# A hybrid decoder step on one core: which place the planner charges for a large tile, and four PSUM banks in turn for the side work

## The chip, the cores and the metric

The kernel runs on one core of one Trainium2 chip. The metric is the device time of one execution in microseconds (us). Lower is better.

## What is computed

Two decoder layers run over 1,024 prompt tokens and 64 sample tokens (8 sequences of 8), in 32-bit floats. The model width is 1,024 and each of the four branches is 512 wide. Cut to what matters, one layer is:

```python
h = rmsnorm(x, norm_w[l])
proj = h @ w_in[l]          # a_x a_b a_c a_z  s_u s_z  c_q c_f c_i c_z  d_q d_k d_v d_z d_r  m_logit
y_a = a_b * short_conv(a_c * a_x, st_conv[l], conv_w[l]) * silu(a_z)
y_s, h_r, h_i = s5_ssm(s_u, ...)                 # 32 groups, 64 complex states each, scan over time
sg = gelu(y_s)
y_b = sg * sigmoid(sg @ w_glu[l] + b_glu[l]) * silu(s_z)
o_c, S_c = gated_recurrence(q_c, k_c, v_c, logf_c, st_hg[l])      # HGRN2, 4 heads, chunks of 64
y_c = rmsnorm(o_c, hgrn_norm[l]) * silu(c_z)
o_d, S_d = gated_recurrence(q_d, k_d, v_d, gk, st_gla[l])         # GLA, 4 heads
y_d = rmsnorm(o_d, gla_norm[l]) * silu(d_z)
p = einsum('blnw,nwd->blnd', stack([y_a, y_b, y_c, y_d]), w_branch[l])
x = x + sum_n(sigmoid(m_logit) * p) @ w_out[l]
```

A final RMSNorm follows, and all end states of the branches are outputs too.

## The kernel before

**Products.** A 32-bit product is made of three TensorE matmuls over operands split into a high and a low part (high times high, low times high, high times low): `xh`, `xl` or `hi`, `lo` on one side, `whi`, `wlo` on the other. ACT makes the high part and DVE the low part. TensorE thus is the engine with by far the most work. A *unit* is one block of 128 output columns over all 1,088 tokens: `unit` runs it as two halves, each of which is 4 accumulations of 272 tokens in two PSUM banks, 48 matmuls over the model width or 24 over a branch's. In the first part of a layer the units go in pairs with seven block products in place of eight (`pair`, names `xc`, `top`, `spot`, `wsum`); the merge gate's pairs are the last of these.

**Stages of a layer.** Projections for the convolution and for S5 (early units and pairs), then the gate pairs, under which the S5 lane runs in four rounds. Then the heads in the order `ORDER = 'H0 H1 H2 H3 G0 G1'`, under which the two recurrences run. Then the merge, in the order `STAGES = '0 2 U 1 3'`: the branch products of the convolution and of HGRN2, the half-GLU of S5 (`U`), the branch products of S5 and of GLA; then `out_proj`. In the profiled execution the gate pairs with the S5 lane lie at about 350 to 760 us (layer 0) and 1840 to 2270 us (layer 1), the heads and the merge at 760 to 1350 and 2270 to 2865 us.

**Lanes.** Everything that is not a unit's matmul is written as generators, the lanes `aux`, `s5l`, `tabs` and `rec`. At each `yield` a lane says when its operands are ready, how many PSUM banks the next step takes (`nsm`), how many large tiles (`need`) and a condition.

**What sets the order.** The program is written once by a planner. `Book` keeps an account of when each engine is free and when each tile was last written and read; `enter` adds a price for every instruction. Between two matmuls of a unit, `Trunk.pump` asks each lane whether its next step is ready by the account, whether the PSUM banks are free by the account (`bank`), whether enough large tiles are left (`fits`), and whether DVE's account is no more than `backlog` ahead of TensorE's (12 us, in the gate pairs 0.5 us). If so the step is written there, and stands in each engine's queue at that place. What the account has wrong becomes a wait on the chip, since every engine works through its own queue in order.

**Places.** Large tiles (128 x 1088 words) come from a pool `big` of `NBIG = 38` places. Before, the account does not know which place a new tile takes: a tile whose place is still being read is written as if it were free. The PSUM has 8 banks: two single ones for the lanes (tag `sm`) and three pairs for the units (tag `mm`).

**Names in the rows.** One helper records every instruction, so nearly all rows of the trace have line L88, and tiles tell them apart. In an S5 round, POOL makes `tm<-Ppow,s5b`, then `et<-tm`, twice, then small products `qp`, `qt` and a memset of `tm`; DVE makes `tm<-Ppow,s5pk` and `gt<-tm`, later copies `tm<-s5b`; TensorE transposes `et` (copied out to `E`) and multiplies `sm<-s5b,tm` and `sm<-gt,tm`, later `sm<-H,gt` and `sm<-apad,E`. In the recurrences `pr`, `prh`, `prl`, `prs`, `att`, `k`, `Tb` and `apad` belong to the decay and attention steps, `osq`, `sqh`, `sql` to the norm of a head's output `o`. In the merge `y` is a branch's output, `g` the gate and `mg` the sum; `yv` and its parts `xh`, `xl` feed the half-GLU.

Of the kernel before, what the change touches and what calls it, by code (L numbers as in the profile page):

```python
# [9 lines left out]
F32 = mybir.dt.float32  # L10
# [16 lines left out]
NBIG = 38  # L27
# [17 lines left out]
WBUF = 5  # L45
KEEP = 5
SPARE5 = 6
LEAD = 0.7


TURNS = (-2, 5, 11)
# [8 lines left out]
SEM = 0.05  # L60
# [36 lines left out]
class Book:  # L97
    def __init__(self, nc):
        self.nc = nc
        self.free = dict.fromkeys(("pe", "act", "dve", "pool", "sp", "dma"), 0.0)  # L100
        self.wr, self.rd = {}, {}
        self.table = None
        for attr, key in (("tensor", "pe"), ("scalar", "act"), ("vector", "dve"), ("gpsimd", "pool"), ("sync", "sp")):
            setattr(self, attr, Meter(self, getattr(nc, attr), key))

    def enter(self, key, op, aps, func):
        out, ins = aps[0], aps[1:]
        n = 1
        for d in max((x.shape[1:] for x in aps), key=lambda d: math.prod(d)):
            n *= d  # L110
        free, us = self.free, 1e-3
        parts = [self.parts_of(x) for x in aps]
        wr = [max(self.wr.get(k, 0.0) for k in p) for p in parts]
        rd = [max(self.rd.get(k, 0.0) for k in p) for p in parts]
        start = max([free[key]] + [t + SEM for t in wr[1:]])

        if key == "pe":
            start = max(start, rd[0] + SEM)
        else:
            start = max(start, rd[0] + SEM, wr[0] + SEM if op != "dma_start" else 0.0)  # L120
        if op == "dma_start":
            free[key] = start + (0.75 if key == "pool" else 0.45)
            size = math.prod(out.shape) * 4.0
            free["dma"] = max(free["dma"], free[key]) + size / 350e3
            end = free["dma"] + 1.9
        else:
            if key == "pe":
                m = math.prod(aps[-1].shape[1:]) if op == "matmul" else 128
                c = (m / 2400 + 0.011 if aps[1].dtype == F32R else 2 * max(m / 1200 + 0.004, 0.109)
                     if op == "matmul" else 0.11)  # L130
            elif key == "act":
                c = 0.155 + n * 0.87 * us
                if func in TABLED and func != self.table:
                    self.table = func
                    c += 1.3
            elif key == "dve":
                c = 0.15 + n * 1.05 * us
            else:
                c = 0.4 if n < 128 else 0.15 + n * (2.4 if op.startswith("tensor_t") or op in ("tensor_mul", "tensor_add", "tensor_sub")
                               else 0.9) * us  # L140
            free[key] = end = start + c
        for p in parts[1:]:
            for k in p:
                self.rd[k] = max(self.rd.get(k, 0.0), end)
        for k in parts[0]:
            self.wr[k] = end

    @staticmethod
    def parts_of(x):

        n = x.name
        if n[:2] not in ("xh", "xl", "hi", "lo", "sp") or getattr(x, "offset", None) is None:
            return (n,)
        a, size = x.offset % T, math.prod(x.shape[1:])
        return ((n,) if a < HT else ()) + ((n + "b",) if a + size > HT else ())
# [16 lines left out]
class Trunk:  # L172
    def __init__(self, ctx, tc, a, o):
# [9 lines left out]
        self.n = 0  # L183
        self.lanes = []
        self.banks = []
        self.alive = set()
        self.keep = KEEP
        self.backlog = BACKLOG
        self.inside = None
# [17 lines left out]

    def bank(self, n):

        names = self.banks[-2:][:n]  # L210
        return max([max(self.nc.rd.get(x, 0.0), self.nc.wr.get(x, 0.0)) + SEM for x in names] + [0.0])

    def free(self, *aps):
        for x in aps:
            self.alive.discard(x.name)

    def fits(self, ln):
        if ln.when and not ln.when():
# [3 lines left out]
    def pump(self):  # L222
        again = True
        while again:
            again = False
            self.weights()
            for ln in self.lanes:
                if (ln.q and ln.ready <= self.now and self.bank(ln.nsm) <= self.now and self.fits(ln)
                        and self.nc.free["dve"] <= self.now + self.backlog):
                    self.stage(ln)  # L230
                    again = True
                    break
# [33 lines left out]
    def big(self, shape, dt=F32, name="b"):  # L266
        n = 1
# [6 lines left out]
        v = t[:shape[0], :n]  # L274
        self.alive.add(v.name)
        assert len(self.alive) <= NBIG, sorted(self.alive)
        if len(shape) == 2:
            return v
        names = "abcdef"[: len(shape) - 1]
        return v.rearrange(f"p ({' '.join(names)}) -> p {' '.join(names)}", **dict(zip(names, shape[1:])))  # L280

    def sm(self):
        t = self.ps.tile([128, 512], F32, tag="sm", name=self.nm("sm"))
        self.banks.append(t[:].name)
        return t

    def mm(self):
        return self.ps.tile([128, 2, 512], F32, tag="mm", name=self.nm("mm"), bufs=3)

    @staticmethod  # L290
    def cut(t, span, nb):
# [61 lines left out]
    def parts_by(self, j):  # L353
# [38 lines left out]
                src = a22  # L392
                drop = [e + 2]

        old = self.places[-WBUF:][0] if len(self.places) >= WBUF else ()
        yield 1, max([self.at(src[:])] + [nc.rd.get(x, 0.0) + SEM for x in old])
        hi = self.wp.tile([128, 4, 128], F32R, tag="whi", name=self.nm("whi"), bufs=WBUF)
        lo = self.wp.tile([128, 4, 128], F32R, tag="wlo", name=self.nm("wlo"), bufs=WBUF)
        self.places.append((hi[:].name, lo[:].name))
        h, lv, r = hi[:], lo[:], src[:]  # L400
        if perm in (1, 2):
            h, lv = (x.rearrange("q k (p g) -> q k g p", g=8) for x in (h, lv))
# [311 lines left out]
    def make_plan(self):  # L714
        self.plan, self.seq = [], []
        self.loaded, self.done, self.raws, self.ws, self.sums_ = set(), set(), {}, {}, {}
        self.nraw = self.di = self.wi = 0
        self.preps, self.places = [], []
        self.merging = False
        self.left = [0.0] * RAWS  # L720

# [411 lines left out]
    def recurrence(self, l, nh, q, f, k, v, vs, sz, y_dst, nw_col, s0, sp_out, ss_out, gate=None):  # L1133
# [24 lines left out]
            Ah = [(A[:, hh, :], hs) for hh, hs in enumerate(heads)]  # L1158
            self.free(q)
        B = k  # L1160
        yield self.at(*own[1]), 0
        own, ready = self.parts(own, cuts, heads)
        yield ready, 1, 1

# [48 lines left out]
        for _ in adv:  # L1213
            pass
        self.free(f)
        yield self.at(*pair[1]), 0
        pair, ready = self.parts(pair, cuts, heads)
        yield ready, 1
        for hh, hs in enumerate(heads):
# [149 lines left out]
        for hh in range(nh):  # L1369
# [22 lines left out]
            for c in cuts:  # L1392
                nc.vector.tensor_mul(sq[:, c], o[:, c], o[:, c])
                nc.scalar.activation(hi[:, c], o[:, c], AF.Square)
            yield self.at(hi), 0
            _, ready = self.parts((sq, (hi, lo)), cuts, heads[:1] if nh == 1 else [slice(0, 128)])
            self.alive.add(sq.name)
            yield ready, 1
            for s, n in SP:
                p = self.sm()  # L1400
# [5 lines left out]
            if len(sz) <= hh:  # L1406
                yield 0.0, 0, 0, lambda: len(sz) > hh
            nc.scalar.activation(sq, sq, AF.Exp, scale=-0.5)
            yield self.at(sq), 0
            nc.vector.tensor_mul(o, o, sq)  # L1410
            nc.vector.scalar_tensor_tensor(o, o, self.cols[:, nw_col:nw_col + 1], sz[hh], op0=ALU.mult, op1=ALU.mult)
            yield self.at(o), 0
# [6 lines left out]
    def gla_gate(self, l, pr):  # L1419
# [22 lines left out]
            yield 0.0, 1  # L1442
        nc.scalar.activation(f, f, AF.Exp, scale=-1.0)
        nc.scalar.activation(f, f, AF.Ln, bias=self.ones[:])
        yield self.at(f), 0
        nc.vector.tensor_sub(f, m, f)
        nc.scalar.activation(f, f, AF.Exp, scale=1.0 / 16.0)
        self.free(m)
# [770 lines left out]
    def layer(self, l):  # L2219
# [38 lines left out]
        self.keep = KEEP  # L2258
        self.backlog = BACKLOG
        self.more = True  # L2260
        for op in ORDER.split():
            i = int(op[1:] or 0)
            if op[0] == "H":
                self.hgrn_units(l, i)
            elif op[0] == "m":
                if i not in sum(early, []):
                    self.gate_unit(l, i)
            else:
                self.gla_units(l, i)
        self.merge(l)  # L2270
        self.mg_h = self.mg
        self.out_proj(l)

# [41 lines left out]
```

## Time and profile before

| | us |
|---|---|
| median of 3 runs | 3059.04 (3057.76 to 3060.28) |
| the profiled execution | 3063.25 |
| span of its trace | 3061.3 |
| busy in it: TensorE | 2947.9 (96%) |
| busy in it: DVE | 1931.8 (63%) |
| busy in it: ACT | 1110.3 (36%) |
| busy in it: POOL | 389.6 (13%) |

All rows below come from the profiled execution, which took 4.2 us more than the median. In the rows, PE is TensorE, PEld its weight loads; "PEclk" is the clock that the throttle granted to TensorE as a share of 2.4 GHz, so that 0.50 is the lower of its two levels (1.2 GHz). In a timeline a row is a start, a busy time, the instruction, the number of merged instructions, and in brackets the idle time of the engine before it and what ended that.

### The profile page before, as it was taken

The numbers are of one execution on the slowest core, as the hardware profiler recorded it, in microseconds if no ns is written. First come the engines' busy times: TensorE is split into PE (matmuls) and PEld (weight loads), VectorE is DVE, ScalarE is ACT, GpSimd is POOL, SyncE is SP. The second block draws the span as 40 slices with busy tenths as digits, with TensorE's granted clock in tenths as the row PEclk, the third lists the DMA queues.
The fourth block names the chain that finished last, engine by engine and source line by source line (L and its number), as shares of the span: only waits on it lengthen the run. The fifth ranks groups of instructions, "written<-read, shape, count | busy, mean of one in ns | idle before, by whom it ended". The sixth has DMA issues, their size and how long they took to land.

```text
span 3061.3 us, 55591 instructions
## 1 busy us (share of the span) xinstructions
PE 2947.9 (96%) x22890; PEld 2862.4 (94%) x22890; DVE 1931.8 (63%) x3396; ACT 1110.3 (36%) x1932; POOL 389.6 (13%) x432
## 2 busy tenths in 40 slices
PE   7999999999999999989999999999999999999998
PEld 6999899999999999989889999999899999999997
DVE  5776676775656466868455666777645565577662
ACT  5332433333333426243343243333333344344321
POOL 2000202220000020213010002211100000103120
PEclk9999999999999999999999999999999999999999
DMA  4422333334212115435233223333421221245332
GB/s 119 162 71 61 101 111 107 106 97 143 61 47 66 40 39 183 153 102 195 88 128 107 62 72 118 100 102 110 162 63 47 63 67 37 75 160 159 133 136 89
DMA packets 318609, 309.41 MB, mean 101 GB/s; under 512 B 18497, under 2 KB 269649, under 8 KB 318357
## 3 DMA queue, kind: packets, MB, share of 16 engines
q1 hardware_dynamic: 316516, 302.02, 31.3%
q0 software_dynamic: 1840, 3.86, 0.4%
q8 instruction: 180, 2.95, 0.4%
q14 instruction: 73, 0.59, 0.1%
HBM read 217.16 MB, written 88.65 MB: 100 GB/s over the span
## 4 chain that ended last, share of the span: by engine, by line
PE 81%; DVE 7%; issue 4%; ACT 3%; DMA 2%; POOL 1%; SPq 1%; DVEq 0%; POOLq 0%; ACTq 0%
PE mm L88 70%; PE sm L88 11%; DVE wlo L88 1%; SPq L88 1%; ACT whi L88 1%; DMA apad<-usc 1%; DVE att L88 1%; DVE spot L88 1%; POOL et L88 1%; POOL tm L88 0%; DVE yb L88 0%; ACT L88 0%; DMA s5b<-in_s_b_im_dram 0%; DVE gt L88 0%; DVE wsum L88 0%
## 5 line engine op out<-in xcount | busy, mean ns | idle before, releaser
L88 PE MATMUL mm<-xc,whi 128*128 128x272 f32 x3136 | 526.7, 290 | 8.9 <-DVE spot L88 7.9
L88 PEld LDWEIGHTS mm<-xc,whi 128*128 128x128 f32 x3136 | 445.4, 191 | 12.7 <-issue 5.8
L88 DVE TENSOR_TENSOR wlo<-wraw,whi 128x512 fp32r<-128x512 f32 x400 | 315.8, 792 | 215.4 <-ACT whi L88 214.4
L88 PE MATMUL mm<-hi,whi 128*128 128x272 f32 (+2 forms) x1928 | 410.9, 293 | 12.5 <-ACT hi L88 4.3
L88 PE MATMUL mm<-lo,whi 128*128 128x272 f32 (+2 forms) x1928 | 409.5, 292 | 4.8 <-DVE lo L88 4.8
L88 PE MATMUL mm<-hi,wlo 128*128 128x272 f32 (+2 forms) x1928 | 409.2, 292 | 0.4 <-DVE wlo L88 0.4
L88 PE MATMUL mm<-xh,whi 128*128 128x272 f32 (+1 forms) x1720 | 370.5, 295 | 9.1 <-ACT spot L88 3.4
L88 PE MATMUL mm<-xl,whi 128*128 128x272 f32 (+1 forms) x1720 | 367.3, 293 | 11.7 <-DVE xl L88 11.7
L88 PE MATMUL mm<-xh,wlo 128*128 128x272 f32 (+1 forms) x1720 | 367.8, 294 | 3.4 <-DVE wlo L88 3.4
L88 ACT ACTIVATE whi<-wraw 128x512 fp32r<-128x512 f32 x400 | 272.8, 686 | 155.9 <-PE mm L88 124.2
L88 PE MATMUL mm<-xc,wlo 128*128 128x272 f32 x1568 | 326.6, 290 | 0.0
L88 PEld LDWEIGHTS mm<-hi,whi 128*128 128x128 f32 x1928 | 306.8, 191 | 15.8 <-issue 5.2
L88 PEld LDWEIGHTS mm<-lo,whi 128*128 128x128 f32 x1928 | 306.5, 191 | 7.1 <-DVE lo L88 5.8
L88 PEld LDWEIGHTS mm<-hi,wlo 128*128 128x128 f32 x1928 | 306.0, 191 | 2.6 <-issue 1.2
L88 PEld LDWEIGHTS mm<-xl,whi 128*128 128x128 f32 x1720 | 274.4, 191 | 13.4 <-DVE xl L88 12.7
L88 PEld LDWEIGHTS mm<-xh,whi 128*128 128x128 f32 x1720 | 274.3, 191 | 12.4 <-ACT whi L88 3.9
L88 PEld LDWEIGHTS mm<-xh,wlo 128*128 128x128 f32 x1720 | 273.9, 191 | 6.5 <-DVE wlo L88 5.3
L88 PEld LDWEIGHTS mm<-xc,wlo 128*128 128x128 f32 x1568 | 247.6, 190 | 0.7 <-issue 0.7
L88 ACT ACTIVATE whi<-wsum 128x512 fp32r<-128x512 f32 x147 | 99.4, 677 | 205.3 <-DVE wsum L88 172.1
L88 DVE TENSOR_TENSOR spot<-spot,mm 128x544 f32<-128x544 f32 x181 | 129.6, 716 | 53.3 <-PE mm L88 50.7
L88 ACT ACTIVATE spot<-spot 128x544 f32<-128x544 f32 x87 | 57.4, 660 | 266.2 <-DVE spot L88 264.6
L88 DVE TENSOR_TENSOR wlo<-wsum,whi 128x512 fp32r<-128x512 f32 x147 | 114.1, 776 | 54.5 <-ACT whi L88 53.3
(367 smaller groups left out, 5162.9 us busy)
## 6 DMA issues: line engine op xcount, KB each, us to landing
wraw<-in_w_in_dram SPq DMA_DIRECT2D x328, 256.0 KB
g<-gsc SPq DMA_DIRECT2D x64, 544.0 KB
gsc<-spot SPq DMA_DIRECT2D x116, 272.0 KB
y<-ysc SPq DMA_DIRECT2D x24, 544.0 KB
wraw<-in_w_branch_dram SPq DMA_DIRECT2D x48, 256.0 KB
ysc<-o SPq DMA_DIRECT2D x16, 544.0 KB
wo<-in_w_out_dram SPq DMA_DIRECT2D x16, 512.0 KB
out_dram<-S SPq DMA_DIRECT2D x12, 512.0 KB
```

Source lines behind the costliest of these rows:

```text
L88: r = fn(*a, **kw)
```

## The change

It has four parts. *Prices*: in `enter`, a DMA into a tile with rows under 64 elements is charged eight times its size, a small POOL operation 0.55 instead of 0.4, and a `mm` tile is kept in the account by halves. *Places*: a list `gone` holds the tiles that were freed; `big` takes the least recently used of them and gives the new tile its time of last use, and `pump` holds a lane back until `places(ln.need)` has passed. *Ahead*: four yields of the recurrence name a time `AHEAD = 1.0` us earlier than the ACT result that they wait for. *Four banks*: from the first head to the end of the merge, `sm()` goes round four banks: two of `sm`, then the two halves of one `mm` tile; outside of that the lanes have their two as before.

```diff
@@ enter, parts_of
+        self.turn += 1
+        for x in aps:
+            self.used[x.name] = self.turn
...
-            size = math.prod(out.shape) * 4.0
+            size = math.prod(out.shape) * 4.0 * (8 if out.shape[-1] < 64 else 1)
...
-                c = 0.4 if n < 128 else 0.15 + n * (2.4 if op.startswith("tensor_t") or op in ("tensor_mul", "tensor_add", "tensor_sub")
+                c = 0.55 if n < 128 else 0.15 + n * (2.4 if op.startswith("tensor_t") or op in ("tensor_mul", "tensor_add", "tensor_sub")
...
+        if n[:2] == "mm" and getattr(x, "offset", None) is not None:
+            a = x.offset % 1024
+            return ((n,) if a < 512 else ()) + ((n + "b",) if a + math.prod(x.shape[1:]) > 512 else ())
@@ bank, free, places, pump
-        names = self.banks[-2:][:n]
-        return max([max(self.nc.rd.get(x, 0.0), self.nc.wr.get(x, 0.0)) + SEM for x in names] + [0.0])
+        names = []
+        while len(names) < n:
+
+            i = (self.nsm + len(names)) % 4 if self.four else 0
+            if i < 2:
+                names.append(self.banks[-2:][len([x for x in names if x[:2] == "sm"]) % 2] if len(self.banks) > 1 else "")
+            else:
+                names.append(self.oldest_mm() if i == 2 or not self.halves else "")
+        return max([self.left_at(x) for x in names] + [0.0])
...
-            self.alive.discard(x.name)
+            if x.name in self.alive:
+                self.alive.discard(x.name)
+                self.gone.append(x.name)
...
+        return max([self.left_at(x) for x in sorted(self.gone, key=lambda x: self.nc.used.get(x, 0))[:n]])
...
+                        and self.places(ln.need) <= self.now
@@ big, sm
+        old = min(self.gone, key=lambda x: self.nc.used.get(x, 0))
+        self.gone.remove(old)
+        self.nc.rd[v.name] = self.nc.rd[v.name + "b"] = self.left_at(old)
+        self.nc.used[v.name] = self.nc.turn
...
+        if self.four:
+            self.nsm += 1
+            if (self.nsm - 1) % 4 == 2:
+                t = self.mm()
+                self.halves = [t[:, 0], t[:, 1]]
+            if (self.nsm - 1) % 4 > 1:
+                return self.halves.pop(0)
@@ recurrence, gla_gate (four places)
-        yield self.at(*own[1]), 0
+        yield self.at(*own[1]) - AHEAD, 0
@@ layer
+        self.four, self.nsm = True, 0
         for op in ORDER.split():
...
         self.merge(l)
+        self.four, self.halves = False, []
```

The instructions are the same ones; their order on each engine differs from the S5 stage of layer 0 on. Three places show how.

DVE in the gate pairs of layer 0, at the start of the second S5 round, before: the round's end `s5pk` and the first work on the new round's `tm`.

```order
L88 TENSOR_TENSOR s5pk_3869<-fs_5222,f_617_5223 128x4x8 x2
L88 TENSOR_TENSOR spot_3390<-spot_3853,mm_5130 128x544
L88 TENSOR_TENSOR wlo_5212<-wsum_5143,whi_5211 128x512
L88 TENSOR_TENSOR wraw_5071<-wraw_4864,wraw_5071 128x512
L88 TENSOR_TENSOR wlo_5271<-wraw_5071,whi_5270 128x512
L88 TENSOR_TENSOR tm_5291<-Ppow,s5pk_3869 128x512 x2
```

The same stretch of DVE after:

```order
L89 TENSOR_TENSOR s5pk_3892<-fs_5320,f_626_5321 128x4x8 x2
L89 TENSOR_TENSOR wlo_5400<-wraw_5116,whi_5399 128x512
L89 TENSOR_TENSOR spot_3853<-spot_1560,mm_5333 128x544
L89 TENSOR_TENSOR wsum_5443<-wraw_5314,wraw_5395 128x512
L89 TENSOR_TENSOR wsum_5444<-wsum_5443,wraw_5116 128x512
L89 TENSOR_TENSOR spot_3853<-spot_3853,mm_5418 128x544
L89 TENSOR_TENSOR spot_3852<-spot_1560,mm_5333 128x544
L89 TENSOR_TENSOR wlo_5453<-wsum_5444,whi_5452 128x512
L89 TENSOR_TENSOR wlo_5466<-wraw_5397,whi_5465 128x512
L89 TENSOR_TENSOR wlo_5498<-wsum_5443,whi_5497 128x512
L89 TENSOR_TENSOR tm_5366<-Ppow,s5pk_3892 128x512 x2
```

Nine steps of the pairs instead of four now stand ahead of the `tm` step that needs POOL's `et`. On TensorE, 186 matmuls of the pairs instead of 76 now stand between the last `sm<-H,gt` of the round before and the first `sm<-s5b,tm` of this one; in the next two rounds 162 and 150 instead of 58 and 50, and the same in layer 1 (186, 162 and 146 instead of 76, 58 and 50). In round one, DVE's `s5tmp<-s5b,zfac` moved back past 54 matmuls of the pairs in both layers.

DVE ahead of the half-GLU in layer 1, before: the last head's norm (`osq`, `sql`), the parts `xl` of `yv`, and the merge's `g` and `mg`.

```order
L88 TENSOR_TENSOR osq_29931<-o_29910 128x320
L88 TENSOR_TENSOR xl_29855<-yv_29614,xh_29854 128x1088
L88 TENSOR_TENSOR yv_29614<-yv_29614,sz_29622 128x1088
L88 TENSOR_TENSOR g_29736<-g_29736,mm_29893 128x544
L88 TENSOR_TENSOR wlo_29977<-wraw_29542,whi_29976 128x4x8x16
L88 TENSOR_TENSOR sql_29933<-osq_29931,sqh_29932 128x384 x2
L88 TENSOR_TENSOR sql_29933<-osq_29931,sqh_29932 128x320
L88 TENSOR_TENSOR xl_29974<-yv_29616,xh_29973 128x1088
```

The same parts after:

```order
L89 TENSOR_TENSOR xl_29700<-yv_29621,xh_29699 128x1088
L89 TENSOR_TENSOR yv_29621<-yv_29621,sz_29629 128x1088
L89 TENSOR_TENSOR g_29551<-g_29551,mm_29706 128x544
L89 TENSOR_TENSOR xl_29737<-yv_29623,xh_29736 128x1088
L89 TENSOR_TENSOR yv_29623<-yv_29623,sz_29631 128x1088
L89 TENSOR_TENSOR wlo_29757<-wraw_29439,whi_29756 128x4x8x16
L89 TENSOR_TENSOR g_29551<-g_29551,mm_29741 128x544
L89 TENSOR_TENSOR mg_28961<-mg_28961,g_29485 128x544
L89 TENSOR_TENSOR xl_29774<-yv_29625,xh_29773 128x1088
```

The norm's steps no longer stand between the `xl`; they come earlier, and so do the `xl` themselves, by about 50 matmuls.

DVE at the start of the merge of layer 1, before: the low parts `lo` of the first branch's output, and what stands between them.

```order
L88 TENSOR_TENSOR lo_28494<-y_28412,hi_28493 128x1088
L88 TENSOR_TENSOR wlo_28498<-wraw_28221,whi_28497 128x512
L88 TENSOR_TENSOR o_28333<-o_28333,osq_28355 128x1088
L88 SCALAR_TENSOR_TENSOR o_28333<-o_28333,cols,sz_27327 128x1088
L88 TENSOR_TENSOR lo_28518<-y_28414,hi_28517 128x1088
L88 TENSOR_TENSOR lo_28534<-y_28416,hi_28533 128x1088
L88 TENSOR_TENSOR lo_28550<-y_28418,hi_28549 128x1088
```

The same place after:

```order
L89 TENSOR_TENSOR lo_28472<-y_28345,hi_28471 128x1088
L89 TENSOR_TENSOR att_28475<-mm_28476,ident 128x512 x2
L89 TENSOR_TENSOR att_28475<-sm_28481,ident 64x64
L89 TENSOR_TENSOR att_28484<-sm_28485,ident 128x512
L89 TENSOR_TENSOR att_28484<-mm_28488,ident 128x512
L89 TENSOR_TENSOR att_28484<-mm_28488,ident 64x64
L89 TENSOR_TENSOR pr_28494<-apad,k_27592 64x544 x2
L89 TENSOR_TENSOR apad<-apad,f_28240 64x544
L89 TENSOR_TENSOR k_27592<-k_27592,f_28240 128x544
L89 TENSOR_TENSOR Tb_28493<-f_28240 128x544
L89 TENSOR_TENSOR lo_28519<-y_28347,hi_28518 128x1088
```

A whole step of the last recurrence now stands ahead of the fourth `lo`, and it reads `mm` banks that the lane has borrowed. Over both layers, the heads and the merge open 85 more `mm` tiles than before (41 in layer 0, 44 in layer 1): these are the lent ones.

## Rows read from the trace of the kernel before

**Rows 1.** The page's busy time by engine: us, share, instructions.

```profile
PE 2947.9 (96%) x22890; PEld 2862.4 (94%) x22890; DVE 1931.8 (63%) x3396; ACT 1110.3 (36%) x1932; POOL 389.6 (13%) x432
```

**Rows 2.** Windows: length, busy PE, PEld, DVE, ACT, POOL, PEclk, DMA share, GB/s.

```profile
350.00:760.00 410.00, 387.23 (x3191) 380.87 (x3190) 276.73 (x603) 133.55 (x258) 76.09 (x108) 0.97 0.37 115
760.00:1350.00 590.00, 576.05 (x4629) 561.44 (x4627) 368.98 (x618) 239.18 (x417) 59.95 (x45) 0.99 0.27 84
1840.00:2270.00 430.00, 405.63 (x3318) 399.21 (x3317) 285.72 (x619) 139.82 (x267) 75.97 (x108) 0.97 0.37 113
```

**Rows 3.** Waits of TensorE over the whole span: us, times, longest.

```profile
PE sm L88 <- DVE tm L88: 16.8, 4, 4.4
PE mm L88 <- DVE spot L88: 14.3, 6, 3.9
PE mm L88 <- DVE xl L88: 11.7, 4, 3.7
PE sm L88 <- ACT E L88: 6.4, 2, 3.2
...
PE sm L88 <- DMA apad<-usc: 5.3, 5, 1.9
PE sm L88 <- DVE att L88: 5.1, 12, 0.9
PE mm L88 <- DVE lo L88: 4.8, 2, 2.4
...
PE sm L88 <- POOL et L88: 3.1, 2, 1.6
```

**Rows 4.** Timeline of POOL, second S5 round of layer 0.

```profile
474.48 1.29 POOL L88 TENSOR_TENSOR et<-tm 128x512 f32<-128x512 f32 x1 [5.35 <-issue]
...
487.57 0.40 POOL L88 MEMSET tm<- 128x368 f32 x1
```

**Rows 5.** Timeline of DVE there.

```profile
479.33 1.29 DVE L88 TENSOR_TENSOR tm<-Ppow,s5pk 128x512 f32<-128x512 f32 x2 [5.46 <-POOL et L88]
```

**Rows 6.** Timeline of TensorE there.

```profile
488.69 0.62 PE L88 MATMUL sm<-s5b,tm 128*32 128x16 f32 x4 [4.04 <-DVE tm L88]
...
490.74 1.28 PE L88 MATMUL mm<-xc,whi 128*128 128x272 f32 x4
...
498.45 0.67 PE L88 MATMUL mm<-xc,whi 128*128 128x272 f32 x4
...
499.20 0.67 PE L88 MATMUL mm<-xc,whi 128*128 128x272 f32 x4
```

**Rows 7.** Timeline of ACT in the third round of layer 0.

```profile
578.25 0.66 ACT L88 ACTIVATE spot<-spot 128x544 f32<-128x544 f32 x1 [9.55 <-DVE spot L88]
```

**Rows 8.** Timeline of DVE in the first round of layer 0.

```profile
365.14 0.42 DVE L88 TENSOR_TENSOR s5tmp<-s5b,zfac 128x256 f32<-128x256 f32 x1 [3.67 <-DMA s5b<-in_s_b_im_dram]
```

**Rows 9.** Windows: the eight half-clock stretches of the S5 stages, their sum.

```profile
sum 47.60, PE 38.58 PEld 36.33 DVE 29.32 ACT 15.30 POOL 9.24; mean PE 4.82 PEld 4.54 DVE 3.66 ACT 1.91 POOL 1.16
```

**Rows 10.** Timeline of DVE ahead of the half-GLU, layer 0.

```profile
1316.11 1.41 DVE L88 TENSOR_TENSOR sql<-osq,sqh 128x384 fp32r<-128x384 f32 x3
```

**Rows 11.** Windows: sum of the two half-clock stretches behind the xl waits.

```profile
sum 13.60, PE 9.41 PEld 8.88 DVE 7.38 ACT 6.82 POOL 0.00; mean PE 4.71 PEld 4.44 DVE 3.69 ACT 3.41 POOL 0.00
```

**Rows 12.** Timeline of DVE at the start of the merge of layer 1.

```profile
2693.60 3.69 DVE L88 TENSOR_TENSOR lo<-y,hi 128x1088 fp32r<-128x1088 f32 x3
...
2719.80 1.28 DVE L88 TENSOR_TENSOR att<-sm,ident 128x512 f32<-128x512 f32 x2
...
2725.28 1.46 DVE L88 TENSOR_TENSOR pr<-apad,k 64x544 f32<-64x544 f32 x2
...
2727.41 2.16 DVE L88 TENSOR_TENSOR k<-k,f 128x544 f32<-128x544 f32 x1
```

**Rows 13.** Windows: a half-clock stretch in the heads of layer 0.

```profile
1129.20:1132.60 3.40, 3.40 (x16) 3.21 (x15) 1.76 (x3) 0.68 (x4) 3.00 (x3) 0.50 0.00 0
```

**Rows 14.** Timeline of TensorE ahead of that stretch.

```profile
1126.86 1.91 PE L88 MATMUL sm<-apad,S 128*128 128x16 f32 x16
```

More of the change, by code (lines that the diff above doesn't have):

```diff
@@ L48 @@
 LEAD = 0.7
+AHEAD = 1.0
 TURNS = (-2, 5, 11)
@@ L101, in __init__ @@
         self.wr, self.rd = {}, {}
+        self.turn, self.used = 0, {}
         self.table = None
@@ L185, in __init__ @@
         self.banks = []
+        self.mms, self.halves, self.nsm, self.four = [], [], 0, False
         self.alive = set()
+        self.gone = [f"none{i}" for i in range(NBIG)]
         self.keep = KEEP
@@ L208, in bank, with oldest_mm, left_at, places @@
     def bank(self, n):
-        names = self.banks[-2:][:n]
-        return max([max(self.nc.rd.get(x, 0.0), self.nc.wr.get(x, 0.0)) + SEM for x in names] + [0.0])
+        names = []
[6 more added lines that the diff above has]
+        return max([self.left_at(x) for x in names] + [0.0])
+    def oldest_mm(self):
+        return min(self.mms[-3:], key=lambda x: self.nc.used.get(x, 0))
     def free(self, *aps):
         for x in aps:
-            self.alive.discard(x.name)
+            if x.name in self.alive:
+                self.alive.discard(x.name)
+                self.gone.append(x.name)
+    def left_at(self, x):
+        return max(d.get(k, 0.0) for d in (self.nc.rd, self.nc.wr) for k in (x, x + "b")) + SEM
+    def places(self, n):
+        if not n:
+            return 0.0
+        return max([self.left_at(x) for x in sorted(self.gone, key=lambda x: self.nc.used.get(x, 0))[:n]])
     def fits(self, ln):
@@ L287, in mm @@
     def mm(self):
-        return self.ps.tile([128, 2, 512], F32, tag="mm", name=self.nm("mm"), bufs=3)
+        t = self.ps.tile([128, 2, 512], F32, tag="mm", name=self.nm("mm"), bufs=3)
+        self.mms.append(t[:].name)
+        return t
     @staticmethod
@@ L393, in parts_by @@
                 drop = [e + 2]
-        old = self.places[-WBUF:][0] if len(self.places) >= WBUF else ()
+        old = self.pairs_[-WBUF:][0] if len(self.pairs_) >= WBUF else ()
         yield 1, max([self.at(src[:])] + [nc.rd.get(x, 0.0) + SEM for x in old])
@@ L398, in parts_by @@
         lo = self.wp.tile([128, 4, 128], F32R, tag="wlo", name=self.nm("wlo"), bufs=WBUF)
-        self.places.append((hi[:].name, lo[:].name))
+        self.pairs_.append((hi[:].name, lo[:].name))
         h, lv, r = hi[:], lo[:], src[:]
@@ L717, in make_plan @@
         self.nraw = self.di = self.wi = 0
-        self.preps, self.places = [], []
+        self.preps, self.pairs_ = [], []
         self.merging = False
@@ L1215, in recurrence @@
         self.free(f)
-        yield self.at(*pair[1]), 0
+        yield self.at(*pair[1]) - AHEAD, 0
         pair, ready = self.parts(pair, cuts, heads)
@@ L1394, in recurrence @@
                 nc.scalar.activation(hi[:, c], o[:, c], AF.Square)
-            yield self.at(hi), 0
+            yield self.at(hi) - AHEAD, 0
             _, ready = self.parts((sq, (hi, lo)), cuts, heads[:1] if nh == 1 else [slice(0, 128)])
             self.alive.add(sq.name)
+            self.gone.remove(sq.name)
             yield ready, 1
@@ L1408, in recurrence @@
             nc.scalar.activation(sq, sq, AF.Exp, scale=-0.5)
-            yield self.at(sq), 0
+            yield self.at(sq) - AHEAD, 0
             nc.vector.tensor_mul(o, o, sq)
@@ L1444, in gla_gate @@
         nc.scalar.activation(f, f, AF.Ln, bias=self.ones[:])
-        yield self.at(f), 0
+        yield self.at(f) - AHEAD, 0
         nc.vector.tensor_sub(f, m, f)
```

## The prediction

> **What bounds the kernel.** I read the busy times first: TensorE is busy for 2947.9 of 3061.3 us [rows 1], so apart from work that the change does not touch, only its idle time and its slow-clock time can be won: some 113 us idle and the stretches at the lower clock. The windows by stage show where these lie: in the two S5 stages TensorE is busy for 387.2 of 410 and 405.6 of 430 us at a mean clock of 0.97, while the heads and the merge of layer 0, with as many lane steps, have 576.1 of 590 at 0.99 [rows 2]. Third, the waits of TensorE by releaser [rows 3]: `tm`, `spot`, `E` and `et` are all waits of the S5 stages, `xl` is the half-GLU, `lo` the start of the merge, `att` the recurrences.
>
> The timelines of one S5 round tell why. POOL starts `et` at 474.48 though it has no row ahead of it for 5.35 us [rows 4]: that is just when TensorE has finished the last `sm<-H,gt`, the old `gt` whose place the new `et` takes. From there POOL's chain runs without a break to the memset at 487.57 to 487.97, DVE's `tm` step stands at the head of its queue for 5.46 us until `et` is through [rows 5], and TensorE stands for 4.04 us before `sm<-s5b,tm` at 488.69 [rows 6]. So from the release of the place to that matmul 14.2 us go by. In the third round the same DVE block keeps `spot` from ACT for 9.55 us [rows 7], and TensorE waits first for the `spot` step that frees a PSUM pair, then for `E`. In the first round DVE stands 3.67 us for a DMA [rows 8], and two `spot` waits follow.
>
> Each wait of over 2 us is followed by the lower clock: behind the 4.04 us four matmuls take 1.28 us at 490.74 and 0.67 at 498.45 [rows 6], and the eight such stretches of the two S5 stages come to 47.6 us with 38.58 us of matmuls in them [rows 9].
>
> **The change, part by part.** *Places and prices in the S5 stage.* Nothing is removed; the question is whether enough of the pairs' work now stands between the release of the place and its users. At full clock six matmuls of a pair take 0.75 us (498.45 to 499.20 [rows 6]), 0.125 each. Before, 76, 58 and 50 matmuls stood between the last `sm<-H,gt` and `sm<-s5b,tm`: 9.5, 7.3 and 6.3 us against a chain of 14.2. After, by the order, 186, 162 and 150 (146 in layer 1): 23, 20 and 18 us. Even if the place came no earlier, the chain would be done 4 us ahead of need. DVE's `tm` step now stands some 88 matmuls (11 us) behind that same release, and POOL's second `et`, which it waits for, ended 4.8 us after it (479.3 against 474.48). The block on DVE should thus go, and with it what was queued there: `spot`, then ACT's `spot` and `E`. In round one `s5tmp` goes back by 54 matmuls, 6.7 us, more than the 3.67 us of its wait. The DMA itself cannot start earlier, since POOL's queue is as it was ahead of it. So I take out all of `tm` 16.8, `spot` 14.3, `E` 6.4 and `et` 3.1: 40.6 us. The half-clock stretches behind them go with them: half of the 38.58 us, 19.3 us. The five `apad<-usc` waits (5.3 us) stay, for the distance to their DMA is as before. What is late next in the stage is a wait of that size.
>
> *The four banks, the gain.* The recurrences move on in longer runs and end sooner. The last head's norm no longer stands among the `xl`; before, three `sql` (1.41 us) stood right ahead of one [rows 10]. I take out the `xl` waits, 11.7 us, and half of the 9.41 us of matmuls in the two stretches behind them [rows 11], 4.7 us. The gains are 76.3 us.
>
> *The four banks, the price.* (a) The start of the merge of layer 1: the fourth `lo` now stands behind a whole `att` step: two pairs of `att` (1.28 us each), two `pr` (1.46), `k` (2.16) [rows 12] and two half-width steps at half a `pr` pair (0.73), 7.6 us. That `lo` is needed 18 matmuls or 2.25 us after the first, so TensorE waits 5.4 us where `lo` now costs 2.4 (4.8 in two [rows 3]): 3.0 us more. Layer 0 stays. (b) A lent bank takes one of the three pairs from the units: the next unit must then wait for the drain of a tile one turn younger. No row shows this in the merge; the bounds are zero (DVE is busy for 369 of 590 us there [rows 2], and a drain is one step over 544 columns, as one `pr`: 0.73 us) and, as the nearest row of a unit that waits for its pair to be drained, a `spot` wait, 14.3 us in six or 2.4 us each [rows 3], with half of a 3.4 us stretch behind it, 4.1 in all. By the order three tiles come within 25 matmuls of their drain with other DVE or ACT steps queued ahead (two in layer 0, in the last heads and the first branch; one in layer 1); I price these at 4.1 and the rest at nothing: 12.3 us. Below nothing is not excluded, since twelve `att` waits (5.1 us) are waits of lanes that four banks could shorten; I count none of it. (c) Longer runs of small lane matmuls: a stretch at half clock without a wait ahead of it stands in the heads, behind a run of lane matmuls, sixteen of them of 16 columns in 1.91 us [rows 13, 14]; it cost half of its 3.40 us. One more per layer: 3.4 us. (d) Nothing says that the S5 stage becomes free of other waits. I leave it as much as the lanes of the heads now wait for `att`, 5.1 us [rows 3]. Together 23.8 us.
>
> *A step named 1 us early* (`AHEAD`) moves DVE steps closer to the ACT result that they need. If DVE stands the full 1 us at each, what is queued behind it are drains and low parts of the units, and these have room as long as DVE is a third idle [rows 2]; I count nothing. If DVE had no slack (at the merge's start), it would be part of (a).
>
> The sum: 76.3 less 23.8 is 52.5 us. 3063.25 less 52.5 is 3010.75 for an execution like the profiled one. That one stood 4.2 us over the median, so I predict 3006.55, **3007 us**.
>
> The page "TensorE: Matmul & The Clock Gate" of the Trainium skill, in "A second HAM failure mode: psum-queue depth-cycling", speaks against the four banks: it tells of a kernel that cycled through PSUM banks, whose TensorE idled briefly between groups of matmuls and so went back and forth between its two clock levels. Here the heads and the merge already go round three pairs and two banks at a mean clock of 0.99 [rows 2], so the trace does not show it yet; by that rule the four banks would bring the first or the second rival below.
>
> **The rivals.** *Lent banks cost everywhere.* Each of the 85 lent tiles costs what a short wait for a lane's bank costs now, 5.1 us in twelve or 0.43 us [rows 3]: 36 us in place of the 12.3 under (b). That gives 3031 us. For it: the halves of a merge unit are 24 matmuls, 3 us, and a drain often stands behind two or three DVE steps of 1.3 us. Against it: the planner holds a lane back until the account has the lent bank free.
>
> *Units starve (slower).* If the account is wrong about drains in the merge as it was about POOL in the S5 stage, units wait the full 2.4 us and the clock falls behind each. At 4.1 us the gain of 52.5 is gone when 16 of the 85 are hit rather than three (64.8 over 4.1); at 25 the price is 102 us, and the time 3097. For it: waits of this kind stand in the trace with just that size. Against it: DVE has a third of its time idle in that stage, in the S5 stage it was blocked.
>
> *The S5 waits come back elsewhere.* The place is released in time, but the later steps of a round now meet other work; the S5 lane ends later and overlaps the first heads. If half of the 59.9 us comes back as other waits, 3037. For it: DVE's queue in that stage is allowed only 0.5 us of lead, so a small error of the account is a wait. Against it: the distances above exceed the chain by 4 to 9 us. The strong form, that the change does not do what it says, would need the new tiles to go to other places than the account supposes; the order shows the users far enough back even then.
>
> *No price at all.* If (a) to (d) come to nothing, 3063.25 less 76.3 less 4.2: 2983.
>
> **How the numbers follow.** Forecast 0.57 (2995 to 3020); lent banks everywhere 0.17; S5 waits back 0.10; no price 0.10; starving units 0.06, of which a little falls near the old time. The range of 8 in 10 reaches from 2986, near the case without a price, to 3038, past the two dearer cases. A measurement of this kernel tells some 0.2%, 6 us, from no change: faster by more 0.91, within it 0.03, slower 0.06.
>
> **What would show it.** In the S5 windows: TensorE waits for `tm`, `spot`, `E` and `et` gone or under 3 us a layer, mean clock 0.99, a stage shorter by 30 us (20 of waits and 10 of the clock); POOL's `et` still starting at the last `sm<-H,gt`, but DVE never standing for it. No `xl` wait ahead of the half-GLU. At the start of layer 1's merge a wait for `lo` or `hi` of about 5 us. In the heads and the merge: waits of `mm<-...` matmuls for `g`, `mg`, `att` or `v` in few places. The forecast is wrong if these are many, if the clock there falls below 0.98, or if the S5 windows still show over 10 us of idle TensorE per layer.

## Result: 0.6% slower, and the profile after

The changed kernel took 3080.22 us (median of 4, 3076.52 to 3081.5) against 3059.66 us for the kernel before: ratio 1.0063, 95% interval 1.0046 to 1.0081. The forecast was 3007 us. Its profiled execution took 3081.2 us, its span is 3079.4 us. The page's busy times, to be held against [rows 1]:

```profile
PE 2954.2 (96%) x22890; PEld 2863.1 (93%) x22890; DVE 1949.4 (63%) x3396; ACT 1093.1 (35%) x1918; POOL 390.0 (13%) x432
```

TensorE stands still for 125 us instead of 113 and is busy 6 us longer. The stages say more. Here are windows of the changed kernel whose bounds are the starts of the same six matmuls as in the table below them: the S5 stage, the heads and the merge of layer 0, then of layer 1 (columns as in [rows 2]):

```profile
351.60:708.00 356.40, 353.48 (x2995) 349.40 (x2995) 259.98 (x535) 125.63 (x240) 63.92 (x100) 1.00 0.41 128
708.00:1135.60 427.60, 404.03 (x3244) 390.55 (x3243) 241.38 (x471) 148.87 (x296) 39.26 (x35) 0.99 0.17 48
1135.60:1354.70 219.10, 205.50 (x1599) 199.65 (x1598) 155.87 (x219) 93.99 (x136) 32.61 (x19) 0.98 0.43 139
1832.70:2206.00 373.30, 367.46 (x3097) 362.69 (x3096) 272.89 (x560) 132.52 (x246) 66.55 (x100) 1.00 0.41 125
2206.00:2671.00 465.00, 440.86 (x3480) 426.98 (x3479) 252.78 (x486) 160.47 (x323) 39.06 (x35) 0.97 0.17 49
2671.00:2932.30 261.30, 242.04 (x1863) 235.63 (x1862) 176.73 (x244) 94.90 (x131) 46.57 (x26) 0.97 0.46 152
```

Length of each stage, in us, in the profiled executions of the kernels before and after and of four of the experiments below:

| | S5, layer 0 | heads 0 | merge 0 | S5, layer 1 | heads 1 | merge 1 |
|---|---|---|---|---|---|---|
| before | 390.2 | 391.4 | 223.3 | 407.4 | 419.1 | 256.4 |
| after | 356.4 | 427.6 | 219.1 | 373.3 | 465.0 | 261.3 |
| e1, no four banks | 358.3 | 392.8 | 219.0 | 370.5 | 422.0 | 252.8 |
| e2, four banks alone | 391.2 | 428.4 | 228.5 | 405.0 | 454.9 | 262.7 |
| e9, same order, own tiles | 358.8 | 399.6 | 207.8 | 371.0 | 424.0 | 249.3 |
| e11, four in the heads alone, own tiles | 357.9 | 399.4 | 204.8 | 369.5 | 425.5 | 243.8 |

The S5 stages gained 33.8 and 34.1 us, and their mean clock rose from 0.97 to 1.00. All of it, and 14 us more, went in the heads (36.2 and 45.9 us longer). Here are the heads of both layers before, at the same bounds:

```profile
740.30:1131.70 391.40, 388.48 (x3167) 378.99 (x3166) 215.17 (x398) 142.02 (x283) 30.49 (x27) 1.00 0.18 50
2238.50:2657.70 419.20, 416.68 (x3402) 406.88 (x3401) 229.77 (x421) 155.58 (x308) 31.91 (x27) 1.00 0.18 51
```

Their clock fell from 1.00 to 0.99 and 0.97. They also hold 77 and 78 more matmuls than before: lane work moved into them, from the S5 stages (37 and 36 fewer) and from the merges (38 and 41 fewer). So the lengths of two stages are not a gain and a loss in full; experiment 9, with the same order of instructions, tells the two apart: against it, the heads of the changed kernel are 28.0 and 41.0 us longer, and its merges 11.3 and 12.0 us. The waits of TensorE over the whole span (columns as in [rows 3]):

```profile
PE mm L89 <- DVE att L89: 34.7, 26, 3.8
PE mm L89 <- DVE S L89: 13.4, 12, 2.7
PE mm L89 <- DVE g L89: 6.3, 5, 2.0
PE mm L89 <- ACT osq L89: 6.1, 8, 0.9
...
PE sm L89 <- DMA apad<-usc: 5.5, 6, 1.7
...
PE mm L89 <- ACT kd L89: 4.9, 7, 0.7
...
PE mm L89 <- DVE mg L89: 2.7, 1, 2.7
PE mm L89 <- DVE Tb L89: 2.2, 5, 0.8
...
PE mm L89 <- DVE spot L89: 0.2, 1, 0.2
```

Of [rows 3], `tm`, `E`, `et` and `xl` are gone and `spot` is down from 14.3 to 0.2. In their place stand waits of lane matmuls that write a lent `mm` bank, for `att`, `S`, `osq`, `kd` and `Tb`: steps of the same lane. The waits for `g` and `mg` are those of units.

The second S5 round of layer 0 shows the gain, in one row each of POOL, DVE and TensorE, to be held against [rows 4 to 6]:

```profile
477.11 1.29 POOL L89 TENSOR_TENSOR et<-tm 128x512 f32<-128x512 f32 x1 [2.67 <-issue]
```

```profile
488.12 1.29 DVE L89 TENSOR_TENSOR tm<-Ppow,s5pk 128x512 f32<-128x512 f32 x2
```

```profile
501.00 0.30 PE L89 MATMUL sm<-s5b,tm 128*32 128x16 f32 x4
```

POOL still stands until the last reader of the old place, but DVE comes 11.0 us later and does not stand, and TensorE comes to `s5b,tm` 23.9 us after the release without a wait; the sum had 11 and 23.

The loss is seen best at one place in the heads of layer 0. TensorE, then DVE:

```profile
1069.83 0.63 PE L89 MATMUL sm<-prs,ones_r 128*128 128x512 f32 x2
1070.30 0.18 PE L89 MATMUL mm<-prs,ones_r 128*64 128x32 f32 x1
1072.80 0.29 PE L89 MATMUL mm<-prs,ones_r 128*64 128x32 f32 x1 [2.33 <-DVE att L89]
1072.93 0.80 PE L89 MATMUL mm<-xh,whi 128*128 128x272 f32 x2
```

```profile
1070.26 2.42 DVE L89 COPY_PREDICATED att<-mask,sm 128x512 f32<-128x512 int32 x2 [3.41 <-PE sm L89]
1072.50 0.25 DVE L89 COPY_PREDICATED att<-mask,mm 64x32 f32<-64x32 int32 x1
1073.13 0.22 DVE L89 COPY_PREDICATED att<-mask,mm 64x32 f32<-64x32 int32 x1 [0.38 <-PE mm L89]
```

Two small matmuls write the two halves, that is the two banks, of one lent tile. The second starts at 1072.80, 0.05 us after DVE has finished reading the first half (1072.50 to 1072.75), though it writes another bank. The compiled program says the same: these are the rows of TensorE there, with their semaphore waits.

```
L89 MATMUL mm_11715<-prs_11607,ones_r 64x32 [waits PE_49]
L89 MATMUL mm_11715<-prs_11607,ones_r 64x32 [waits DVE_49]
```

The value that the second waits for is the one that DVE's copy out of the first half raises. The order between engines is thus kept by tile, not by bank, while the planner's account had been changed to keep a `mm` tile by halves. I went through all lane matmuls of the program in this way: 87 write one half and wait for a reader of the other; in the trace 72 of them stand, for 68.8 us in all. Behind some of these waits the clock falls. The heads and the merge have fourteen half-clock stretches: twelve begin within 3 us of such a wait, two behind a unit's wait for `mg` or `g`; behind most of the 72 waits there is none. These are the longest of the fourteen and their sum:

```profile
2479.10:2496.20 17.10, 17.10 (x80) 16.74 (x79) 7.83 (x15) 0.00 (x0) 0.00 (x0) 0.50 0.06 15
...
sum 68.10, PE 65.84 PEld 64.14 DVE 32.96 ACT 13.89 POOL 13.70; mean PE 4.70 PEld 4.58 DVE 2.35 ACT 0.99 POOL 0.98
```

Half of the 65.8 us of matmuls, 33 us by this estimate, is lost to the clock there.

On such waits the page "PSUM — Partial Sum Buffer" of the Trainium skill, under "PSUM bank collisions raise a hardware error", asks for a guard by bank and quadrant. By that rule a matmul into the second bank needs no wait for a reader of the first; the wait here is the program's, not the chip's, and the ninth experiment, in which the two banks belong to two tiles, agrees.

### The profile page after: what moved, and what is told of

The parts are those of the page before. It is cut to its first block, busy times and chain, and to the rows that moved or that the text cites. A ratio compares the mean times of both kernels' runs of the same rounds, so it can differ in the third digit from the quotient of the medians.

```text
span 3079.4 us, 55560 instructions
## 1 busy us (share of the span) xinstructions
PE 2954.2 (96%) x22890; PEld 2863.1 (93%) x22890; DVE 1949.4 (63%) x3396; ACT 1093.1 (35%) x1918; POOL 390.0 (13%) x432
## 5 line engine op out<-in xcount | busy, mean ns | idle before, releaser
L89 PE MATMUL mm<-xc,whi 128*128 128x272 f32 x3136 | 519.7, 288 | 1.2 <-ACT xc L89 0.8
```

Source lines behind the costliest of these rows:

```text
L89: r = fn(*a, **kw)
```

## Experiments

Each run was timed against the kernel before on the same chip. Theory A says that the waits on the other half of the lent tile, with the clock behind them, ate the gain.

**1. The change without the four banks.**

```diff
-        self.four, self.nsm = True, 0
+        self.four, self.nsm = False, 0
```

> The changed kernel without the four banks: prices, places and AHEAD stay, lanes keep their two own banks. In the changed kernel 72 waits with 68.8 us stand at matmuls that write the second half of a lent tile while DVE or ACT still reads the first half. Theory A (these waits, and the slow clock behind them, ate the gain): without lent tiles the S5 stages keep their 68 us (33.9 and 34.1), the heads and the merge go back to about their time before, plus some 10 us of S5 lane work that now falls into the heads; the xl waits may come back (16 us). Forecast 2990 to 3005 us. Rival B (the new pace of the S5 stage only moves its waits into the heads and the merge): 3050 to 3080 us, with waits in the heads that do not belong to lent tiles.

Measured: 2992.63 us, ratio 0.9772 (0.9757 to 0.9786). The S5 gain stands, the heads are within 3 us of before, and of TensorE's waits `xl` is back and `att` is a wait of 0.4 us for an own bank again:

```profile
PE mm L89 <- DVE xl L89: 12.2, 4, 3.2
...
PE sm L89 <- DVE att L89: 4.5, 11, 0.8
```

So the four banks cost 88 us, and rival B falls.

**2. The four banks alone.** Prices, `places` and `AHEAD` back to those of before; the four banks stay, and with them the account of a `mm` tile by halves.

```diff
-            size = math.prod(out.shape) * 4.0 * (8 if out.shape[-1] < 64 else 1)
+            size = math.prod(out.shape) * 4.0
-                c = 0.55 if n < 128 else ...
+                c = 0.4 if n < 128 else ...
-                        and self.places(ln.need) <= self.now
-        self.nc.rd[v.name] = self.nc.rd[v.name + "b"] = self.left_at(old)
-AHEAD = 1.0
+AHEAD = 0.0
```

> The kernel before with the four banks alone: no new prices, no account of places, AHEAD 0. The S5 rounds stand as before (76, 58 and 50 matmuls between place and user) and 78 matmuls wait for a read of the other half of their own lent tile. Theory A: the S5 waits of before (40.6 us) are all there, the xl waits may go (16 us with clock), and the 78 waits at 0.8 us each plus the clock behind them add 62 to 90 us: 3105 to 3135 us. Rival B (the lent tiles cost little by themselves; the loss is the S5 lane's late work meeting the heads): 3045 to 3065 us.

Measured: 3162.01 us, ratio 1.0322 (1.0304 to 1.0339). The direction is A's, the size more than I gave: of the 78 matmuls 72 stood, for 71.2 us, and the waits of the S5 stage are all there.

```profile
PE mm L89 <- DVE att L89: 33.3, 26, 2.6
PE mm L89 <- DVE S L89: 19.7, 14, 2.7
PE sm L89 <- DVE tm L89: 16.9, 4, 4.4
PE mm L89 <- DVE spot L89: 14.4, 6, 3.8
PE mm L89 <- DVE g L89: 10.2, 7, 2.0
```

**3. Each lent bank a tile of its own.** Twice as many pairs are lent, one bank of each unused.

```diff
-            if (self.nsm - 1) % 4 == 2:
-                t = self.mm()
-                self.halves = [t[:, 0], t[:, 1]]
             if (self.nsm - 1) % 4 > 1:
-                return self.halves.pop(0)
+                return self.mm()[:, 0]
```

> The changed kernel, but each lent bank is the first half of a tile of its own, so that no matmul writes into a tile whose other half is being read; twice as many pairs are lent, and one bank of each lies idle. Theory A: the 72 waits are gone and the S5 gain stays: 2990 to 3015 us, and no TensorE wait of lane matmuls for att, S or osq over 1 us. Rival C (the loss is that units have too few pairs left while banks are lent): worse than the changed kernel, 3085 us and more, with waits of unit matmuls for g, mg or sz.

Measured: 2981.47 us, ratio 0.9737 (0.9723 to 0.9752), faster than both kernels and 8.5 us below A's range. Rival C falls: lending twice as many pairs does no harm, if no two lane banks share a tile. (An `att` wait of 1.5 us is left, as the longest of eight.)

**4. Three banks in turn.** As in 3, but `% 3`: two own, one lent.

> The changed kernel with three banks in turn: two own and the first half of one lent tile. No matmul can wait for the other half. Theory A: 2985 to 3010 us, at or a little under the kernel without any lent bank if more banks help the lanes at all. Rival C (too few pairs for the units): about half of the loss of four banks stays, 3035 to 3060 us.

Measured: 2986.02 us, ratio 0.9754 (0.9738 to 0.977). It is in A's range again, and clear of rival C's.

**5. No four banks, no account of places.**

```diff
-                        and self.places(ln.need) <= self.now
-        self.nc.rd[v.name] = self.nc.rd[v.name + "b"] = self.left_at(old)
```

> No four banks, and the account of places off too: prices and AHEAD stay. By the order the S5 rounds have 58, 46 and 100 matmuls of the pairs between the last reader of the old place and its next user (before: 76, 58, 50; without the four banks: 186, 162, 150), and the chain on POOL and DVE takes 14.2 us, or 114 matmuls. Theory D (the account of places made the gain): the tm, et, E and spot waits are back, 3045 to 3070 us. Rival E (the prices of the small POOL steps and of the DMA made it): 2990 to 3005 us.

Measured: 3037.21 us, ratio 0.9925 (0.991 to 0.994): 45 us over experiment 1. The waits of the S5 stage are back in part, with longer single ones where only 46 and 58 matmuls are left, and its S5 stages (389.2 and 395.5 us) are 31 and 25 us longer than in experiment 1:

```profile
PE mm L89 <- DVE spot L89: 21.5, 4, 5.7
PE sm L89 <- DVE tm L89: 14.5, 2, 7.3
```

The account of places makes most of the gain; that it came out under the forecast is not taken apart.

**6. No four banks, the prices of before.**

```diff
-            size = math.prod(out.shape) * 4.0 * (8 if out.shape[-1] < 64 else 1)
+            size = math.prod(out.shape) * 4.0
-                c = 0.55 if n < 128 else ...
+                c = 0.4 if n < 128 else ...
```

> No four banks, and the prices as before: places and AHEAD stay. Rounds of 184, 180 and 133 matmuls (152 in layer 1) between place and user. Theory D: the S5 gain stays but for the DMA wait of s5tmp in round one and the two spot waits behind it (some 5 to 8 us a layer with the clock): 2995 to 3012 us. Rival E: 3040 us or more.

Measured: 2996.83 us, ratio 0.9792 (0.9775 to 0.9809), whose interval meets that of experiment 1. The S5 stages are 5.3 and 5.8 us longer in the trace (363.6 and 376.3), as forecast, and the merges 2.0 and 4.7 us shorter, for a reason that I did not test.

**7. No four banks, `AHEAD` 0.**

> No four banks, AHEAD 0: prices and places stay. Naming a DVE step 1 us early was counted at nothing. If so, within 4 us of the kernel without the four banks: 2989 to 2997 us. If queueing early shortens the recurrences on TensorE, up to 10 us slower; if it holds up drains, up to 10 us faster.

Measured: 3000.15 us, ratio 0.9806 (0.9789 to 0.9822), clear of experiment 1: 7.5 us slower by the medians. The heads and the merge of layer 0 are 3.3 and 5.8 us longer. TensorE's wait for `lo` is what grew, from 0.5 us in two to

```profile
PE mm L89 <- DVE lo L89: 5.4, 4, 2.4
```

So naming a DVE step early is worth something, where I counted nothing. By which way it reaches `lo` I did not test.

**8. The account told the truth.** Four banks and halves as in the change, but a `mm` tile is one thing in the account, and a step that takes the second half waits, in the plan, for the reader of the first.

```diff
-        if n[:2] == "mm" and getattr(x, "offset", None) is not None:
-            a = x.offset % 1024
-            return ((n,) if a < 512 else ()) + ((n + "b",) if a + math.prod(x.shape[1:]) > 512 else ())
...
-                names.append(self.oldest_mm() if i == 2 or not self.halves else "")
+                names.append(self.oldest_mm() if i == 2 or not self.halves else self.halves[0].name)
```

> The changed kernel with four banks and lent tiles in halves, but the account keeps a mm tile as one again, and a step that takes the second half is held back until the account has the first half read. 86 matmuls still carry a wait on a reader of the other half. Theory A with a planner that can put work in between: the waits shrink where the two halves belong to two steps, not where one step takes both: 3010 to 3050 us. If the account's error alone made the waits long: 2985 to 3000 us. If knowing changes nothing: 3070 to 3090 us.

Measured: 3010.96 us, ratio 0.9839 (0.9824 to 0.9853). The 86 waits are still in the program, but only 18 of them stand, for 11.1 us: other work now fills the time. That gets back 69 us of the changed kernel's time. It stays 18 us behind the kernel without four banks, for a reason that was not tested.

**9. The same order, the second half in a tile of its own.** The planner takes the new tile for the second half of the first, so every engine's instructions are those of the changed kernel in the same order; only the bank that 87 matmuls write, and with it their wait, is another.

```diff
                 t = self.mm()
-                self.halves = [t[:, 0], t[:, 1]]
+                u = self.ps.tile([128, 2, 512], F32, tag="mm", name=self.nm("mn"), bufs=3)
+                self.nc.twin[u[:].name] = t[:].name
+                self.halves = [t[:, 0], u[:, 0]]
```

> The changed kernel with every instruction of every engine in its place; only the second half of each lent pair is moved to a tile of its own, which the planner's account still takes for the half of the first. The 87 waits on a reader of the other half are gone, nothing else moves; one more pair is taken from the units at each turn. Theory A: the 68.8 us of waits and nearly all of the clock behind them (the slow stretches of the heads and the merge, some 25 us) go: 2983 to 3005 us. Rival F (the order made with four banks is itself bad: lane steps too early, long runs, drains late): 3040 us or more, with the waits moved to other readers.

Measured: 2983.57 us, ratio 0.9751 (0.9737 to 0.9766): 96.7 us less than the changed kernel with not one instruction moved. The place shown above, now (`mn` is the new tile), TensorE and DVE:

```profile
1049.32 0.63 PE L89 MATMUL sm<-prs,ones_r 128*128 128x512 f32 x2
1049.79 0.18 PE L89 MATMUL mm<-prs,ones_r 128*64 128x32 f32 x1
1049.81 0.21 PE L89 MATMUL mn<-prs,ones_r 128*64 128x32 f32 x1
1049.87 0.50 PE L89 MATMUL mm<-xh,whi 128*128 128x272 f32 x2
```

```profile
1049.75 2.45 DVE L89 COPY_PREDICATED att<-mask,sm 128x512 f32<-128x512 int32 x2 [1.85 <-PE sm L89]
1052.02 0.25 DVE L89 COPY_PREDICATED att<-mask,mm 64x32 f32<-64x32 int32 x1
1052.10 0.24 DVE L89 COPY_PREDICATED att<-mask,mn 64x32 f32<-64x32 int32 x1
```

DVE is as late as before with its first read, at 1052.02, but the second matmul has run 2.2 us ahead of it. The windows of the heads and the merge of layer 1 (424.0 and 249.3 us) have the clock at 1.00 and 0.99:

```profile
2162.10:2586.10 424.00, 422.93 (x3480) 414.56 (x3479) 252.00 (x486) 159.56 (x323) 38.97 (x35) 1.00 0.19 53
2586.10:2835.40 249.30, 235.93 (x1863) 230.31 (x1862) 176.12 (x244) 94.64 (x131) 46.60 (x26) 0.99 0.48 158
```

The page's busy times of this run:

```profile
PE 2915.5 (98%) x22890; PEld 2836.7 (95%) x22890; DVE 1947.5 (65%) x3396; ACT 1089.6 (37%) x1918; POOL 390.6 (13%) x432
```

Of the 96.9 us between the spans of the two traces, 58.2 us are idle time of TensorE (125.2 in the changed kernel, 67.0 here) and 38.7 us busy time. The idle time fell by less than the 68.8 us of waits, because some 10 us of other waits stand that did not before, `att` (7.6 us) and `lo` (2.4 us) among them. Of the busy time some 28 us are the clock in the heads and the merge, where three half-clock stretches of 3.4 us are left of fourteen with 68.1 us; the rest I did not take apart. Since nothing but the tile of the second half differs, this settles the cause; rival F falls.

**10. Own tiles, four banks in the merge alone**, and **11. in the heads alone.** The line that sets `four` is moved behind the heads, or the one that clears it ahead of the merge.

> Four banks, each lent one a tile of its own, in the merge alone; in the heads the lanes keep two. Against the kernel without four banks (2992.6 us), the one with own tiles from the heads on spent 6.7 and 1.8 us more in the heads and 9.7 and 6.3 us less in the merge. If the two stages add up: 2973 to 2979 us. If the merge's gain comes from the lanes having run ahead in the heads (the norm of the last head out of the half-GLU's way): 2986 to 2995 us with the xl waits back.

> The other half: four banks with own tiles in the heads alone, two in the merge. If the stages add up: 2997 to 3003 us. If running ahead in the heads is what helps the merge: 2979 to 2990 us, without the xl waits.

Measured: 2982.45 us, ratio 0.9759 (0.9741 to 0.9776), between the two cases given for 10, and 2976.55 us, ratio 0.9732 (0.9718 to 0.9747), 2.5 us under the second case for 11. With the four banks in the heads alone the merges are the shortest of all (204.8 and 243.8 us), and no `xl` wait of the half-GLU is left: running ahead in the heads is enough to clear the merge. Yet with four banks in the merge alone the `xl` waits shrink too (2.6 us in two), and the median is 10 us under experiment 1, though the intervals meet; so the split is not clean. Between 3, 9, 10 and 11 the intervals overlap.

## Why the prediction was wrong

**Right: what bounds the kernel, and the S5 stage.** The step from "enough of the pairs' work between the place and its users" to "the waits go" held: of the 40.6 us, 0.2 us is left. With the clock the stages are 67.9 us shorter where the sum had 59.9 less 5.1 for what stays; some of the difference is lane work that moved into the heads. Experiment 5 shows that the account of places did most of it. The `apad` waits stayed as said (5.5 us for 5.3), and a new `ys` wait of 2.8 us came. "Each wait of over 2 us is followed by the lower clock" is true of the waits of the S5 stages that it was read from, but not of the whole trace before; no half-clock stretch follows this one:

```profile
1577.29 0.51 PE L88 MATMUL mm<-hi,whi 128*128 128x272 f32 x2 [2.43 <-ACT whi L88]
```

**Right: the half-GLU.** The `xl` waits are gone after the change and back without the four banks (12.2 us), and gone again in experiment 11. With a tile for each bank, four banks are 9 to 16 us faster than none (9, 3 and 11 against 1, the last two clear of the noise), where the sum had 16.4 us of gain.

**Wrong: the price of the four banks.** The step that failed is (b): "A lent bank takes one of the three pairs from the units: the next unit must then wait". I asked only what lending does to the units, and went through the order for unit tiles that come close behind their drain. That effect exists and is about as small as priced: in experiment 9, where the shared tiles are gone, the units wait 6.4 us for `g` and 4.3 us for `att`, against the 12.3 us of (b), 7.2 of them waits. What I did not ask is what sharing a tile does to the lane itself. I took the two halves of a lent tile for two banks, because the account takes them so, and never read the waits that the second half's matmuls carry in the program. They are 68.8 us of waits with some 28 us of clock behind them, and taking them away is worth 96.7 us; the whole price in the sum was 23.8 us. Two of the signs named for a wrong forecast came: the waits of `mm<-...` matmuls are many, and the clock of layer 1's heads is 0.97.

**Wrong in kind: the second rival.** It said "units starve" and priced 25 lent tiles at 4.1 us each, 102 us. The size was near the truth, the mechanism not: after the change units wait 6.3 us for `g` and 2.7 us for `mg`, and experiment 3, which lends twice as many pairs, is faster. The page "TensorE: Matmul & The Clock Gate" of the Trainium skill, under "A second HAM failure mode: psum-queue depth-cycling", did describe the symptom, short waits between groups and a clock that goes back and forth. Here the waits came from shared tiles, and going round four banks with a tile each leaves the clock at 1.00 in the heads.

**A wrong count.** The lent tiles are 105 and not 85: the program opens 610 `mm` tiles in place of 505, and 53 of the lent ones are used in layer 0, 52 in layer 1. The first rival, at 0.43 us for each, would have priced 45 us in place of 36; it is still less than half of what was lost.

**Mis-sized.** (a) The start of the merge of layer 1: 5.4 us of waits were forecast for `lo`; in experiment 9 there are 3.1 us of a lane matmul for `att` and 1.7 us for `lo`, near it by another way. (c) One more half-clock stretch per layer behind long runs of small matmuls: none came with own tiles. `AHEAD` was counted at nothing and is worth some 7.5 us. Leaving out the waits on the other half (experiment 9), the forecast would have been 23 us too high, 2 us outside its own range.

## What to carry to other kernels

When a change hands out parts of one tile as if they were separate buffers, read in the compiled program what the accesses to the second part wait for: here the order was kept by tile, and 87 matmuls waited for a reader of the other bank. A planner's account that is finer than the program's own order hides such waits; making the account coarse again (experiment 8) moves other work into the gap and gets back 69 of some 97 us, and a tile for each bank (3, 9, 11) takes the wait away. A cost of lending a buffer has to be asked at both ends, the lender's and the borrower's.

## What was not expected of the hardware

In layer 1 of the changed kernel a single wait of 1.38 us at 2477.47 was followed by 17.1 us at the lower clock, the row 2479.10 above, though TensorE was busy through all of it. In this time it went through three runs of 16 to 18 lane matmuls of 64 columns (`q,k`) between the units' matmuls. The same matmul of an earlier step waited as long, and no half-clock stretch came behind it:

```profile
2477.47 0.29 PE L89 MATMUL mm<-prs,ones_r 128*64 128x32 f32 x2 [1.38 <-DVE att L89]
```

```profile
2324.99 0.29 PE L89 MATMUL mm<-prs,ones_r 128*64 128x32 f32 x2 [1.38 <-DVE att L89]
```

In experiment 9, with the same order of instructions and no wait there, the heads of layer 1 have no half-clock stretch at all. What decides between the two was not tested.
